# Moved scalings, reordered first transfers and products on ones in a two-layer hybrid decoder kernel

## The chip, the cores and the metric

The kernel runs on one core of one Trainium2 chip. The metric is the device time of one execution in microseconds (us); lower is better. A profiled execution also leaves a trace, whose span runs from the first to the last instruction.

## The reference

Two layers work on h, 272 tokens (16 learned ones and 256 of the input) by 2048 channels in float32:

```python
u = rmsnorm(h, pre_w)
proj = u @ w_in
pool_v, pool_g, z, xbc, dt, q, k, v, g, iq, ik, iw = split(proj)
pool_out = silu(pool_g) * pool_mixer(pool_v)            # windowed means, minus the input, grouped matmul
ssd_out = ssd_mixer(xbc, z, dt)                         # conv, chunked state space, y * silu(z), group norm
attn_out = silu(g) * dsa_attention(q, k, v, iq, ik, iw) # top-64 keys chosen by an index score
mix = concat([pool_out, ssd_out, attn_out])
h = h + rmsnorm(mix @ w_out, post_w)
```

The state-space mixer has 32 heads in 4 groups. Each group's y is gated and normalised by the mean of its squares. The output is the last 256 tokens.

## The kernel before

Channels lie on the 128 partitions and tokens along the free axis. Each weight tile comes by a transfer on SP's queue (`wr`, five buffers) and is split in two halves. For each half ACT writes a high part `wh` (`split`, line 238) and DVE the low part `wl` (line 247); TensorE then makes three products per piece of u, whose own high part is made by ACT (line 397) and low part by DVE (line 399). There are 10 buffers for high and 9 for low parts. The order of all engines' queues is the order in which the Python program issues instructions: every queue is first in, first out.

**The lead.** Layer 0 begins with eight rounds (`hh` 0 to 7) in `lead_0`. Each round multiplies one half quarter of u with three weight halves: a small block `gm` (6 products of 272 columns) and two index-query blocks `g0iq` (12 each of 256). The weight tiles are numbered as they are used: 0, 1, 2 for the first quarter, then 3 (small), 4 and 5 for the second, and so on. x comes in eight pairs of chunks (`load_x(i, k)` loads pair 2i + k/2), and `feed(p)` makes the u parts of pair p; `LEAD` says before which product each is issued. A weight transfer waits until the tile that had its buffer five tiles before has been split. When the lead is done the sums of squares, the row factor, the rotary embedding and the index keys follow in the shade of the next blocks.

**Ticks.** The blocks' products are the backbone. After each quarter of a block `tick()` advances every generator in `gens` by one step; a `yield n` makes a generator sleep for n ticks. Elementwise work is thus put between the products by hand. A block has four ticks of some 2.8 us.

**Index stage.** `EARLIEST` lists what is issued in successive ticks: `K`, `R` and `D` make the index key and bring its lower rows down, `L1` and `L0` (`keys_low`) make its parts, `a` (`iq_1`) evacuates an index-query block with a shuffle and a product (lines 477 and 478), `b`, `h`, `l` finish it, `P` are the score products (line 647).

**Attention head** (`head`): softmax of the two query blocks, after which POOL scales the first 16 columns, replicated, into `lr` (line 779) and the rest in place in `lg` (line 781); TensorE transposes both (lines 786 to 792).

**State-space groups.** A group has five blocks: two `xs`, one `BC`, two `z`, hence 20 ticks. `post_BC` transposes B, makes `bt` (lines 978, 984, 985), and a tick later multiplies it into the states `pst` (line 994); then four `decay` generators make `M` on DVE, ACT and POOL (lines 1016, 1022, 1029), which `ssd_y` needs for `py` (line 1049), after the products `ph` (line 1043). At the end of the group `post_z` sums the squares of y, waits `PNY` ticks, multiplies by ones (`pn`, line 1095), waits a tick, evacuates, waits `PGY` ticks, makes the inverse root on DVE (7 instructions), waits a tick, scales y (line 1104, four instructions), waits a tick and splits the result (`mix_out`). These steps run beside the next group's blocks.

**End.** `out_tokens` multiplies by w_out with tokens on partitions, four strips of 512 columns for each half of the tokens. `post` squares a strip on ACT and scales it on DVE; `finish` makes the root from the four sums and then, strip by strip, adds the residual and stores. The second half's last products are held back, so that the first half's end runs beside them.

Of the kernel before, what the change touches and what calls it, by code (L numbers as in the profile page):

```python
# [10 lines left out]
F32 = mybir.dt.float32  # L11
# [7 lines left out]
P = 128  # L19
# [18 lines left out]
class Plan:  # L38
# [48 lines left out]
QROT = (2, 3, 0, 1)  # L87
PVW = (2, 2, 2, 3)
PLQ, PLQ3 = 2, 4
KY, VEY = 2, 2  # L90

LEAD1 = {("m", 5): "a0", ("m", 7): "f"}
EARLIEST = (
    ("f g", "b0", "K R h0", "a1", "m D l0", "b1 L1", "t L0 h1 a2"),
    ("g", "K R", "b0", "m D h0", "l0 a1", "b1 L1", "t L0 h1 a2"),
)
INDEX = (
# [3 lines left out]
)  # L101
MY = 4
PNY, PGY = 2, 7
VY = 2
XY = 2
LEAD = (
    {(): "f0 s f1", (0, 1): "f2", (0, 2): "f3", (1, 1): "f4", (1, 3): "f5", (2, 2): "f6", (3, 1): "f7"},
)
RY = 4
NX = 4  # L110
# [13 lines left out]
def hybrid(ctx: ExitStack, tc: tile.TileContext, I, out, dbg=None, layers=2):  # L124
# [23 lines left out]
    def rep8(ap):  # L148

        return bc(ap[:, None, :], [ap.shape[0], 8, 16])  # L150

    def by8(ap):
        return ap.rearrange("p (e s) -> p e s", e=8)
# [144 lines left out]
    def rsqrt_v(y, v, w, p):  # L298
# [6 lines left out]
        V.scalar_tensor_tensor(p, p, Q[2], w, op0=OP.add, op1=OP.mult)  # L305
        V.scalar_tensor_tensor(y, p, Q[3], y, op0=OP.add, op1=OP.mult)

    warm = const.tile([P, 1], F32, name="warm")
    V.memset(warm, 0.0)
    A.activation(warm, warm, AF.Copy)  # L310
# [3 lines left out]
    def load_x(eng, i, k):  # L314
        eng.dma_start(hs[i // 2][:, 4 * (i % 2) + k:4 * (i % 2) + k + 2], I["xT"][i, :, k:k + 2])

    def load_half(i, h):

        if not h:
            raws[i] = wraw.tile([P, 4, 256 if i else P], F32, name=f"wr{i}", tag="wr")  # L320
        src = I["wi"][0, i - 1, 0] if i else I["wm"][0, 0]
        nc.sync.dma_start(raws[i][:, 2 * h:2 * h + 2], src[:, 2 * h:2 * h + 2])
        lpos[0] = max(lpos[0], i + 1)

# [2 lines left out]
    for h in range(2):  # L327
        for i in range(1 + NLEAD):
            load_half(i, h)
        if h == 0:  # L330
            load_x(nc.sync, 0, 2)
    nc.sync.dma_start(par[:, 0, 16:], I["par"][:, 0, 16:])
    nc.sync.dma_start(par[:, 1], I["par"][:, 1])
    for i in range(1, 4):
        load_x(nc.sync, i, 0)
        load_x(nc.sync, i, 2)
        load(min(RAWB, 3 + i))
    xpad = []
    for i in range(2):
        t = const.tile([P, 2, 16 + T], F32, name=f"xpad{i}")  # L340
# [4 lines left out]
    ikl = const.tile([P, T], F32R, name="ikl")  # L345
    cst = const.tile([P, 3, P], F32, name="cst")
    ident, tri, tri8 = (cst[:, i] for i in range(3))
    ones_r = const.tile([P, P], F32R, name="ones")
    ones = ones_r.bitcast(F32)
    G.memset(ones, 1.0)  # L350
    dtc = const.tile([P, 2, 2, 32], F32, name="dtc")
    pfix = const.tile([P, 4, 16], F32, name="pfix")
    xpi, xpdone = [0], set()
# [15 lines left out]
    def layer(L, hs):  # L369
# [91 lines left out]
        def early():  # L461

            nc.sync.dma_start(rope, I["rope"])
            if L == 0:
                nc.sync.dma_start(dtc, I["dtc"])
                nc.sync.dma_start(pfix, I["pfix"])
            nc.sync.dma_start(mb, I["mask"])
# [280 lines left out]
        def head(i, c, qr, qs):  # L748
# [27 lines left out]

            lr = pr.tile([P, 3, 128], F32, name="lr", tag="pair")
            for j, (a0, a1, n) in enumerate(segs):
                G.tensor_scalar(by8(lr[0:n, j]), rep8(lg[0:n, a0:a0 + 16]), nm[j][0:n], None, op0=OP.mult)
                if j < 2:  # L780
                    G.tensor_scalar(lg[:, a0 + 16:a1], lg[:, a0 + 16:a1], nm[j], None, op0=OP.mult)
            yield HY
# [282 lines left out]
        def post_z(i, ps):  # L1065
            g, j = i // 2, i % 2
            zg = yield from gate(ps, t0, ("z", i))
            s = sd[g]
            yg = s["yg"]
            for c in (2 * j, 2 * j + 1):  # L1070
                yield from until(f"M{g}_{c}")
            yield 1
            yo = pair("yo")
            ssd_y(g, j, yo)
            yield 1
            V.tensor_tensor(yg[:, 2 * j:2 * j + 2, 16:], yg[:, 2 * j:2 * j + 2, 16:], yo[:, :, 16:], op=OP.add)
            ysl = yg[:, 2 * j:2 * j + 2, t0:]
            V.tensor_tensor(ysl, ysl, zg[:, :, t0:T], op=OP.mult)
            q = pair("ysq")
            A.activation(q[:, :, t0:], ysl, AF.Square)  # L1080
            G.tensor_tensor(q[:, 0, t0:], q[:, 0, t0:], q[:, 1, t0:], op=OP.add)
            if j == 0:
                s["q"] = q
                done.add(f"q{g}")
                return
            done.add(f"y{g}")
            yield from until(f"q{g}")
            qs = pr.tile([P, 2, T], F32R, name="ysr", tag="pair")
            G.tensor_tensor(qs[:, 0, t0:], q[:, 0, t0:], s["q"][:, 0, t0:], op=OP.add)
            G.tensor_tensor(q[:, 0, t0:], q[:, 0, t0:], s["q"][:, 0, t0:], op=OP.add)  # L1090
            G.tensor_tensor(qs[:, 1, t0:], q[:, 0, t0:], qs[:, 0, t0:].bitcast(F32), op=OP.subtract)
            yield PNY
            pn = aux("pn")
            for k in range(2):
                TE.matmul(pn[:, t0:T], ones_r, qs[:, k, t0:], start=k == 0, stop=k == 1)
            yield 1

            rg, v, w_, p_ = (rope[:, k, t0:] for k in range(4))
            V.tensor_scalar(v, pn[:, t0:T], 1.0 / (512 * KQ * KQ), EPS / (KQ * KQ), op0=OP.mult, op1=OP.add)
            yield PGY  # L1100
            rsqrt_v(rg, v, w_, p_)
            yield 1
            for c in range(4):
                V.scalar_tensor_tensor(yg[:, c, t0:], yg[:, c, t0:], pa[:, NW + 4 * g + c:NW + 4 * g + c + 1], rg,
                                       op0=OP.mult, op1=OP.mult)
            dump_m(f"mixS{L}_{g}", yg)
            m = slots.tile([P, 2, 4, T], F32R, name=f"mixS{L}_{g}", tag=f"S{SS[g] if g < 3 else SP_[1]}")
            mixS[g] = m
            yield 1
            mix_out((m, 0), yg[:, :, t0:], t0, 4)  # L1110
            done.add(f"mixS{g}")
# [76 lines left out]
        def lead_0():  # L1188

            lead = [psg.tile([P, 2, 512], F32, name=f"g{L}iq{b}", tag="g") for b in range(2)]  # L1190
            pm = aux(f"gm{L}")
            row["ps"] = aux("psr")
            spawn(squares_0())

            def lead_in(*key):

                for w in LEAD[L].get(key, "").split():
                    if w == "s":
                        split(3, 3)
                    else:  # L1200
                        feed(int(w[1]))

            lead_in()
            for hh in range(8):
                q, half = hh // 2, hh % 2
                lead_in(hh, 0)
                gemm_h([pm], us[q], half, 0, q == 0, q == 3)
                for b in range(NLEAD):
                    lead_in(hh, 1 + b)
                    gemm_h(banks(lead[b]), us[q], half, NM, q == 0, q == 3)  # L1210
                lead_in(hh, 3)
                tick()
                if hh == 1:
                    nc.sync.dma_start(cst, I["cst"])
                if hh == 3:
                    early()
            misc["ps"] = pm
            for b in range(NLEAD):
                iqp[b] = lead[b]
            iq_1(0)  # L1220
            spawn(index_stage())
            spawn(dt_chain())
# [207 lines left out]
    def out_tokens(mixes, SO, SR, done, pool_mm):  # L1430
# [7 lines left out]
        def residual():  # L1438

            for p in range(8):  # L1440
# [8 lines left out]
                for b in range(2):  # L1449
                    A.copy(res[b][:, 256 * p:256 * p + 256], pt[:, 256 * b:256 * b + 256])  # L1450

        def post(n, b, ps):
            j = pair("osq")
            A.activation(j.rearrange("p c t -> p (c t)")[:, 0:512], ps, AF.Square, accum_out=ss[:, b, n:n + 1])
            V.scalar_tensor_tensor(o[b][:, 512 * n:512 * n + 512], ps, KQ * math.sqrt(DM),
                                   pw[n // 2][:, 512 * (n % 2):512 * (n % 2) + 512], op0=OP.mult, op1=OP.mult)

        def partial(b):

# [1 line left out]
            V.tensor_reduce(v, ss[:, b, 0:3], op=OP.add, axis=AX.X)  # L1461
            V.tensor_scalar(v, v, EPS * DM, None, op0=OP.add)

        def finish(b):
            y, v, w, p_ = (tot[:, b, i:i + 1] for i in range(4))
            V.tensor_tensor(v, v, ss[:, b, 3:4], op=OP.add)
            V.tensor_scalar(y.bitcast(I32), v.bitcast(I32), -0.5, RSQ, op0=OP.mult, op1=OP.add)
            V.scalar_tensor_tensor(w, y, y, v, op0=OP.mult, op1=OP.mult)
            V.scalar_tensor_tensor(p_, w, Q[0], w, op0=OP.add, op1=OP.mult)
            V.scalar_tensor_tensor(p_, p_, Q[1], w, op0=OP.add, op1=OP.mult)  # L1470
            V.scalar_tensor_tensor(p_, p_, Q[2], w, op0=OP.add, op1=OP.mult)
            V.scalar_tensor_tensor(y, p_, Q[3], y, op0=OP.add, op1=OP.mult)
            for c0, c1 in ((0, 512), (512, 1024), (1024, 1536), (1536, 2048)):
                x = o[b][:, c0:c1]
                V.scalar_tensor_tensor(x, x, y, res[b][:, c0:c1], op0=OP.mult, op1=OP.add)
                nc.sync.dma_start(out[b, :, c0:c1], x)

        HOLD = HIB - 1
        for n in range(4):
# [32 lines left out]
                continue  # L1512
            while gens:
                tick()
            post(3, 0, o_[0])
            finish(0)
            for i, h in enumerate(held):
                mm_t(o_[1], *h, False, i == len(held) - 1)
            post(3, 1, o_[1])
            finish(1)  # L1520

    split_h = []

# [81 lines left out]
```

## Time and profile before

| | |
|---|---|
| median of 3 runs | 1556.72 us (1556.2 to 1557.01) |
| profiled execution, its own time | 1555.74 us |
| its span | 1554.0 us |
| TensorE busy | 1528.7 us (98%) |
| DVE busy | 1209.7 us (78%) |
| ACT busy | 889.2 us (57%) |
| POOL busy | 229.3 us (15%) |

The span holds all instructions; the 1.7 us around it belong to the execution but to no instruction. Busy shares are means over stages with different limits. A wait in the trace is the idle time of an engine before an instruction, put down to what ended it.

### The profile page before, as it was taken

What the parts mean: (1) busy time and instruction counts of PE and PEld (TensorE: products, weight loads), DVE (VectorE), ACT (ScalarE), POOL (GpSimd) and SP (SyncE); (2) the same over time, 40 slices, a digit from 0 to 9 for tenths busy, and PEclk for the clock granted to TensorE, in tenths of its full rate; (3) what the DMA queues carried; (4) which work ended last, traced back from release to release, by engine and by line L of the source; (5) the groups of instructions that cost most, each with busy time, mean ns of one, the idle gap of its engine ahead of it and who ended that gap; (6) DMA issues with size and microseconds to landing.
All of it is one profiled execution on the core that took longest, in us unless ns stands there. A gap on an engine that the chain in (4) does not pass through costs nothing.

```text
span 1554.0 us, 31057 instructions
## 1 busy us (share of the span) xinstructions
PE 1528.7 (98%) x11788; PEld 1472.2 (95%) x11788; DVE 1209.7 (78%) x2370; ACT 889.2 (57%) x1667; POOL 229.3 (15%) x227
## 2 busy tenths in 40 slices
PE   7999999999999999999999999999999999999997
PEld 7999999999999999999999999999999999988886
DVE  6989777788899978554599898877898989875454
ACT  6455556666667664444455545666667667445542
POOL 0000253221203031000100000532103021300000
PEclk9999999999999999999999999999999999999999
DMA  8545543455454545555536546545454554466652
GB/s 278 192 151 166 174 150 136 158 173 190 136 179 153 189 156 174 206 201 177 176 110 246 180 142 205 162 151 175 167 192 147 194 183 159 164 229 199 217 185 92
DMA packets 78310, 272.44 MB, mean 175 GB/s; under 512 B 8848, under 2 KB 11984, under 8 KB 77136
## 3 DMA queue, kind: packets, MB, share of 16 engines
q1 hardware_dynamic: 78064, 270.39, 51.8%
q8 instruction: 92, 1.51, 0.4%
q14 instruction: 58, 0.48, 0.1%
q10 hardware_dynamic: 96, 0.07, 0.0%
HBM read 266.03 MB, written 4.40 MB: 174 GB/s over the span
## 4 chain that ended last, share of the span: by engine, by line
PE 91%; DVE 4%; issue 2%; POOL 1%; DMA 1%; SPq 0%; ACT 0%; DVEq 0%; ACTq 0%; POOLq 0%
PE go L274 4%; PE go L273 4%; PE go L272 4%; PE got L296 4%; PE got L294 4%; PE got L295 4%; PE g0xs L272 2%; PE g1xs L272 2%; PE g0xs L274 2%; PE g1xs L274 2%; PE g0xs L273 2%; PE g1xs L273 2%; PE g1z L272 2%; PE g1z L274 2%; PE g1z L273 2%
## 5 line engine op out<-in xcount | busy, mean ns | idle before, releaser
L247 DVE TENSOR_TENSOR wl<-wr,wh 128x512 fp32r<-128x512 f32 (+1 forms) x952 | 664.2, 724 | 251.3 <-PE go L274 66.2
L238 ACT CAST wh<-wr 128x512 fp32r<-128x512 f32 (+1 forms) x952 | 564.8, 615 | 404.9 <-PE go L273 88.1
L272 PE MATMUL g0xs<-u,wh 128*128 128x272 f32 x256 | 74.7, 292 | 0.0
L272 PE MATMUL g1xs<-u,wh 128*128 128x272 f32 x256 | 74.6, 291 | 0.0
L272 PE MATMUL g0z<-u,wh 128*128 128x272 f32 x256 | 74.5, 291 | 0.0
L274 PE MATMUL go<-mixS,wl 128*128 128x272 f32 x256 | 74.1, 290 | 0.0
L274 PE MATMUL g0xs<-u,wl 128*128 128x272 f32 x256 | 74.1, 290 | 0.0
L274 PE MATMUL g0z<-u,wl 128*128 128x272 f32 x256 | 74.1, 289 | 0.0
L274 PE MATMUL g1xs<-u,wl 128*128 128x272 f32 x256 | 74.0, 289 | 0.0
L272 PE MATMUL go<-mixS,wh 128*128 128x272 f32 x256 | 74.0, 289 | 0.0
L273 PE MATMUL g0xs<-u,wh 128*128 128x272 f32 x256 | 73.6, 288 | 0.0
L273 PE MATMUL g1xs<-u,wh 128*128 128x272 f32 x256 | 73.6, 287 | 0.0
L273 PE MATMUL go<-mixS,wh 128*128 128x272 f32 x256 | 73.6, 287 | 0.0
L273 PE MATMUL g0z<-u,wh 128*128 128x272 f32 x256 | 73.6, 287 | 0.0
L272 PE MATMUL g1z<-u,wh 128*128 128x256 f32 x256 | 72.7, 284 | 0.0
L274 PE MATMUL g1z<-u,wl 128*128 128x256 f32 x256 | 71.6, 280 | 0.0
L273 PE MATMUL g1z<-u,wh 128*128 128x256 f32 x256 | 71.6, 280 | 0.0
L1029 POOL TENSOR_TENSOR M<-M,cbm 128x512 f32<-128x512 f32 x32 | 50.9, 1591 | 93.0 <-ACT M L1022 93.0
L484 POOL TENSOR_TENSOR ropet<-ropet,rope 128x544 f32<-128x544 f32 (+1 forms) x8 | 10.6, 1327 | 353.0 <-DVE ropet L477 353.0
L1016 DVE TENSOR_SCALAR M<-csb,cs 128x128 f32<-128x128 f32 x128 | 50.9, 446 | 0.0
L294 PE MATMUL got<-wh,mixS 128*128 128x512 f32 x128 | 50.8, 397 | 0.0
L296 PE MATMUL got<-wh,mixS 128*128 128x512 f32 x128 | 50.5, 394 | 0.0
(525 smaller groups left out, 5357.8 us busy)
## 6 DMA issues: line engine op xcount, KB each, us to landing
wr<-wi SPq DMA_DIRECT2D x334, 512.0 KB, 3.3
wr<-wo SPq DMA_DIRECT2D x128, 512.0 KB, 3.4
csb<-csd SPq DMA_DIRECT2D x8, 1088.0 KB, 8.5
x<-xT SPq DMA_DIRECT2D x8, 272.0 KB, 4.7
res<-xT SPq DMA_DIRECT2D x4, 544.0 KB, 6.4
h1d<-o SPq DMA_DIRECT2D x4, 544.0 KB, 6.8
wr<-plw SPq DMA_DIRECT2D x8, 256.0 KB, 2.7
hx<-h1d SPq DMA_DIRECT2D x8, 256.0 KB, 3.7
```

What stands on the lines that cost most here:

```text
L238: A.copy(hi, r[:, 2 * h:2 * h + 2])
L247: V.tensor_tensor(lo, r[:, 2 * h:2 * h + 2], his[i].bitcast(F32), op=OP.subtract)
L272: TE.matmul(o, w_h, u[:, 0, k, t1:T], start=first and k == 0, stop=False)
L273: TE.matmul(o, w_h, u[:, 1, k, t1:T], start=False, stop=False)
L274: TE.matmul(o, w_l, u[:, 0, k, t1:T], start=False, stop=last and k == 3)
L294: TE.matmul(o, m_h, hi, start=first, stop=False)
L295: TE.matmul(o, m_h, lo, start=False, stop=False)
L296: TE.matmul(o, m_l, hi, start=False, stop=last)
L484: e.tensor_tensor(t[:, :nch, c0:T], t[:, :nch, c0:T], bc(rope[:, b + 1:b + 2, c0:T], [P, nch, n]), op=OP.mult)
L1016: V.tensor_scalar(M[:, h, sl], csb[:, h, sl], cs[:, 1 + b, hg:hg + 1], 0.0, op0=OP.subtract, op1=OP.min)
L1029: G.tensor_tensor(M[:, hh, 16:], M[:, hh, 16:], bc(cbm[:, None, 16:], [P, 2, 256]), op=OP.mult)
```

## The change

- Ten products of a 128x128 tile of ones with itself are issued on TensorE first; the tile is made by POOL's first instruction.
- The first transfers come in another order: tiles 3 and 4 come in halves as tiles 0 to 2 do, each pair of x just ahead of its halves; `par`'s larger pieces go behind `rope` in `early()`; pairs 5, 6 and 7 are issued with the parts of `LEAD`, behind tiles 5, 6 and 7.
- In `EARLIEST` `L0` moves one step ahead of `a2`, and `L1` ahead of `b1`.
- The replicated columns `lr` are scaled by DVE instead of POOL.
- `PNY` is 3 instead of 2. `PGY` is 6 instead of 7 for the first three groups and 3 for the last; the scaling then waits 3 ticks (1 for the last) instead of 1. In ticks after the sums of squares: `pn` at 3 (was 2), root at 10 (was 10), scaling at 13 (was 11), split at 14 (was 12); for the last group root at 7, scaling at 8, split at 9.
- At the end the last strip is scaled after the root, just before it is added, and in two halves for the second half of the tokens; the squares are summed as before.

```diff
+WARM = 10
 EARLIEST = (
-    ("f g", "b0", "K R h0", "a1", "m D l0", "b1 L1", "t L0 h1 a2"),
-    ("g", "K R", "b0", "m D h0", "l0 a1", "b1 L1", "t L0 h1 a2"),
+    ("f g", "b0", "K R h0", "a1", "m D l0", "L1 b1 L0", "t h1 a2"),
+    ("g", "K R", "b0", "m D h0", "l0 a1", "L1 b1 L0", "t h1 a2"),
 )
-PNY, PGY = 2, 7
+PNY, PGY, SGY = 3, 6, 3
 LEAD = (
-    {(): "f0 s f1", (0, 1): "f2", (0, 2): "f3", (1, 1): "f4", (1, 3): "f5", (2, 2): "f6", (3, 1): "f7"},
+    {(): "f0 s f1", (0, 1): "f2 x5", (0, 2): "f3 x6 x7", (1, 1): "f4", (1, 3): "f5", (2, 2): "f6", (3, 1): "f7"},
 )
+    ones_r = const.tile([P, P], F32R, name="ones")
+    ones = ones_r.bitcast(F32)
+    G.memset(ones, 1.0)
+
+    pw_ = aux("warm")
+    for _ in range(WARM):
+        TE.matmul(pw_[:, 0:P], ones, ones, start=True, stop=True)
...
-    nc.sync.dma_start(par[:, 0, 16:], I["par"][:, 0, 16:])
-    nc.sync.dma_start(par[:, 1], I["par"][:, 1])
-    for i in range(1, 4):
-        load_x(nc.sync, i, 0)
-        load_x(nc.sync, i, 2)
-        load(min(RAWB, 3 + i))
+    for h in range(2):
+        load_x(nc.sync, 1, 2 * h)
+        for i in range(1 + NLEAD, RAWB):
+            load_half(i, h)
+    load_x(nc.sync, 2, 0)
...
             nc.sync.dma_start(rope, I["rope"])
             if L == 0:
+                nc.sync.dma_start(par[:, 0, 16:], I["par"][:, 0, 16:])
+                nc.sync.dma_start(par[:, 1], I["par"][:, 1])
...
-                G.tensor_scalar(by8(lr[0:n, j]), rep8(lg[0:n, a0:a0 + 16]), nm[j][0:n], None, op0=OP.mult)
+                V.tensor_scalar(by8(lr[0:n, j]), rep8(lg[0:n, a0:a0 + 16]), nm[j][0:n], None, op0=OP.mult)
...
-            yield PGY
+            yield PGY if g < 3 else 3
             rsqrt_v(rg, v, w_, p_)
-            yield 1
+            yield SGY if g < 3 else 1
...
+        def square_t(k, b, ps):
+            j = pair("osq")
+            A.activation(j.rearrange("p c t -> p (c t)")[:, 0:ps.shape[1]], ps, AF.Square, accum_out=ss[:, b, k:k + 1])
+
+        def scale_t(b, ps, c0):
+            c1 = c0 + ps.shape[1]
+            V.scalar_tensor_tensor(o[b][:, c0:c1], ps, KQ * math.sqrt(DM),
+                                   pw[c0 // 1024][:, c0 % 1024:(c1 - 1) % 1024 + 1], op0=OP.mult, op1=OP.mult)
...
-            for c0, c1 in ((0, 512), (512, 1024), (1024, 1536), (1536, 2048)):
+            for c0, c1, ps in strips:
+                if ps is not None:
+                    scale_t(b, ps, c0)
                 x = o[b][:, c0:c1]
...
-            post(3, 0, o_[0])
-            finish(0)
+            whole = [(c, c + 512, None) for c in range(0, 1536, 512)]
+            square_t(3, 0, o_[0])
+            finish(0, 3, whole + [(1536, 2048, o_[0])])
...
-            post(3, 1, o_[1])
-            finish(1)
+            square_t(3, 1, o_[1])
+            finish(1, 3, whole + [(1536, 1792, o_[1][:, 0:256]), (1792, 2048, o_[1][:, 256:512])])
```

## Rows read from the trace of the kernel before

**Rows 1.** The page's first part: busy us (share of the span) xinstructions.

```profile
PE 1528.7 (98%) x11788; PEld 1472.2 (95%) x11788; DVE 1209.7 (78%) x2370; ACT 889.2 (57%) x1667; POOL 229.3 (15%) x227
```

**Rows 2.** Waits of PE: who waited for whom: us in total, times, longest.

```profile
PE gm L272 <- ACT wh L238: 5.9, 1, 5.9
PE pst L994 <- DVE bt L984: 5.4, 6, 1.3
...
PE pt L791 <- POOL lg L781: 0.9, 2, 0.5
PE pq L647 <- DVE ikl L524: 0.6, 1, 0.6
...
PE g1k L272 <- DVE iqr L478: 0.4, 1, 0.4
PE pq L647 <- DVE iqr L478: 0.4, 1, 0.4
PE pn L1095 <- POOL ysr L1091: 0.3, 1, 0.3
```

**Rows 3.** Stretches: length, busy us (xcount) of each engine, clock, DMA share, GB/s.

```profile
5.90:10.70 4.80, 4.76 (x22) 4.77 (x23) 3.62 (x7) 3.78 (x8) 0.00 (x0) 1.00 1.06 381
10.70:17.50 6.80, 6.80 (x58) 6.76 (x57) 3.46 (x7) 2.63 (x7) 0.00 (x0) 1.00 1.03 396
17.50:20.10 2.60, 0.67 (x4) 0.30 (x2) 1.54 (x4) 2.60 (x7) 0.00 (x0) 1.00 0.35 139
20.10:24.40 4.30, 4.28 (x23) 4.28 (x24) 4.10 (x9) 3.76 (x9) 0.00 (x0) 0.60 0.63 158
24.40:40.80 16.40, 16.40 (x139) 16.40 (x139) 14.82 (x27) 12.23 (x24) 0.00 (x0) 1.00 0.85 301
```

**Rows 4.** Timeline: start, us, engine, line, instruction, count [idle before]; the sixth tile.

```profile
17.48 0.62 ACT L238 CAST wh<-wr 128x512 fp32r<-128x512 f32 x1 [2.10 <-DMA wr<-wi]
...
19.39 1.02 DVE L247 TENSOR_TENSOR wl<-wr,wh 128x512 fp32r<-128x512 f32 x2
...
20.12 0.39 PE L274 MATMUL g0iq<-u,wl 128*128 128x256 f32 x1 [1.47 <-DVE wl L247]
```

**Rows 5.** Timeline of DVE and PE where the second layer's second group makes states.

```profile
1161.41 1.67 DVE L1104 SCALAR_TENSOR_TENSOR yg<-yg,par,rope 128x256 f32<-128x256 f32 x4
...
1163.10 0.28 PE L274 MATMUL g1z<-u,wl 128*128 128x256 f32 x1
...
1164.33 0.29 DVE L984 TENSOR_TENSOR bt<-pb,bt 32x128 fp32r<-32x128 f32 x1
...
1164.67 0.50 PE L994 MATMUL pst<-xdd,bt 128*128 128x512 f32 x1 [1.29 <-DVE bt L984]
```

**Rows 6.** Timeline of DVE and PE at the second layer's first score products.

```profile
854.36 0.66 DVE L478 TENSOR_TENSOR iqr<-g1iq,rope 128x512 f32<-128x512 f32 x1
...
855.16 0.36 PE L272 MATMUL g1k<-u,wh 128*128 128x272 f32 x1 [0.44 <-DVE iqr L478]
```

**Rows 7.** Timeline of POOL in an attention head of the second layer.

```profile
1007.61 1.66 POOL L779 TENSOR_SCALAR lr<-lg,nm 128x128 f32<-128x128 f32 x1
1009.25 0.92 POOL L781 TENSOR_SCALAR lg<-lg,nm 128x256 f32<-128x256 f32 x1
```

**Rows 8.** Timeline of DVE, POOL and PE among a group's decays in the second layer.

```profile
1172.43 1.80 DVE L1016 TENSOR_SCALAR M<-csb,cs 128x128 f32<-128x128 f32 x3
...
1172.65 1.31 POOL L1029 TENSOR_TENSOR M<-M,cbm 128x512 f32<-128x512 f32 x1 [5.61 <-ACT M L1022]
...
1183.86 1.28 POOL L1029 TENSOR_TENSOR M<-M,cbm 128x512 f32<-128x512 f32 x1 [3.45 <-ACT M L1022]
...
1188.78 0.61 PE L1043 MATMUL ph<-BC,H 128*128 128x128 f32 x4
```

**Rows 9.** Timeline of DVE at the end.

```profile
1545.58 0.69 DVE L1455 SCALAR_TENSOR_TENSOR ot<-got,pw 128x512 f32<-128x512 f32 x1 [1.50 <-ACT osq L1454]
...
1547.59 2.74 DVE L1475 SCALAR_TENSOR_TENSOR ot<-ot,tot,rt 128x512 f32<-128x512 f32 x4
```

More of the change, by code (lines that the diff above doesn't have):

```diff
@@ L317, in load_half @@
     def load_half(i, h):
+        q, b = divmod(i, 1 + NLEAD)
         if not h:
-            raws[i] = wraw.tile([P, 4, 256 if i else P], F32, name=f"wr{i}", tag="wr")
-        src = I["wi"][0, i - 1, 0] if i else I["wm"][0, 0]
+            raws[i] = wraw.tile([P, 4, 256 if b else P], F32, name=f"wr{i}", tag="wr")
+        src = I["wi"][0, b - 1, q] if b else I["wm"][0, q]
         nc.sync.dma_start(raws[i][:, 2 * h:2 * h + 2], src[:, 2 * h:2 * h + 2])
@@ L347, in hybrid @@
     ident, tri, tri8 = (cst[:, i] for i in range(3))
-    ones_r = const.tile([P, P], F32R, name="ones")
-    ones = ones_r.bitcast(F32)
-    G.memset(ones, 1.0)
     dtc = const.tile([P, 2, 2, 32], F32, name="dtc")
@@ L1199, in lead_in @@
                         split(3, 3)
+                    elif w[0] == "x":
+                        load_x(nc.sync, int(w[1]) // 2, 2 * (int(w[1]) % 2))
                     else:
@@ L1450, in residual @@
                     A.copy(res[b][:, 256 * p:256 * p + 256], pt[:, 256 * b:256 * b + 256])
+        def square_t(k, b, ps):
[5 more added lines that the diff above has]
+                                   pw[c0 // 1024][:, c0 % 1024:(c1 - 1) % 1024 + 1], op0=OP.mult, op1=OP.mult)
         def post(n, b, ps):
[L1453 to L1456, printed above, removed]
+            square_t(n, b, ps)
+            scale_t(b, ps, 512 * n)
         def partial(b):
@@ L1462, in partial, with finish @@
             V.tensor_scalar(v, v, EPS * DM, None, op0=OP.add)
-        def finish(b):
+        def finish(b, k, strips):
             y, v, w, p_ = (tot[:, b, i:i + 1] for i in range(4))
-            V.tensor_tensor(v, v, ss[:, b, 3:4], op=OP.add)
+            V.tensor_tensor(v, v, ss[:, b, k:k + 1], op=OP.add)
             V.tensor_scalar(y.bitcast(I32), v.bitcast(I32), -0.5, RSQ, op0=OP.mult, op1=OP.add)
```

## The prediction

> **What bounds the kernel now.** I read the page first: TensorE is busy 98% of the span and DVE 78% [rows 1]. A busy matmul row includes overlapped time, so I didn't read this as "nothing left"; I asked where TensorE stands still. The list of its waits has nine rows, some 16 us in all; the two of the lead are told by the timeline below, the others are [rows 2]: 5.9 before the first product, 5.4 in six waits of the state product `pst`, and under 1 us each at the head transposes `pt`, the score products `pq`, `g1k` and `pn`. The reader should see that every edit aims at one of these rows.
>
> The waits hide a second loss, the pace. By stretch [rows 3], the lead took 22 matmuls in 4.80 us at first (0.218 us each), 58 in 6.80 (0.117), 23 in 4.30 at a granted clock of 0.60, then 139 in 16.40 (0.118). The first stretch ran at the lower level (1.2 GHz) by its pace, whatever its clock column says (no record stands so early), and the third again mostly at that level, just after 2.60 us in which TensorE was busy for 0.67. The lead's 240 products (8 rounds of 30) take 240 x 0.118 = 28.3 us at the full pace; they took 34.9 (5.9 to 40.8). So 6.6 us are the most that the lead can give.
>
> Why it stood still is in the timeline [rows 4]. ACT waited 2.10 us for a weight transfer and split it at 17.48; the two parts of u that stand next in ACT's and DVE's queues went ahead of its low half, which DVE began at 19.39; TensorE went on at 20.12. DMA was full meanwhile (396 GB/s, share 1.03 [rows 3]), so that transfer was late because of what stood ahead of it.
>
> **Part by part: the start.** The late transfer is the sixth weight tile (`wr5`, block iq1 of the second quarter). Today two pieces of `par` and three x pairs go ahead of it that the change puts behind it: 0.19 MB and 3 x 0.279 MB, 1.03 MB in all. At 396 GB/s that is 2.6 us. Its issue doesn't hold it back: it waits for the buffer of tile 0, whose last reader is among the first splits. So ACT's split moves from 17.48 to about 14.9, and with the same steps behind it (2.64 us from 17.48 to 20.12) TensorE goes on at 17.5. If it then keeps the higher level, the 23 matmuls of 20.1 to 24.4 take 23 x 0.118 = 2.7 instead of 4.3: 1.6 more. DVE's chain moves by 2.6 only and TensorE's by 4.2; I take 0.1 off for low halves that are now just in time: 4.1 us. Bounds: 2.6 (the lower level returns) and 6.6 (no loss at all).
>
> The ten products on ones leave two records each. Four f32 128x128 products are 0.61 us [rows 8], so 20 records are about 3.0 us, some 5.6 at the lower level's pace; begun near 1 us they end, at the worst, 0.7 after the first real product could start (5.9). I cost them at nothing and also give them nothing. With a fast first round TensorE reaches the sixth tile at most 2.2 earlier (22 x 0.1), near 15.3 to 16, and waits there 1.5 to 2.2; with a slow one it arrives near 17.5, as today. Either way it goes on at 17.5. The transfer covers gain and cost; without that cover they would be worth up to 2.2.
>
> On SP the pairs x5, x6, x7 now queue behind tiles 5, 6 and 7, which wait for buffers. Their u parts are used two and more rounds of 3.6 us later; that covers them. The two `par` pieces now go behind `rope`: nothing of them is read in the lead. `rope` keeps its place; weight tiles issued after them are later by two issues, covered by the splits that run ahead.
>
> **Keys.** `keys_low(0)` goes ahead of the ring's next shuffles, and one of the score waits names `ikl`. In the second layer [rows 2, 6] `pq` waits 0.6 for `ikl`, then `g1k` 0.4 for `iqr` L478, the evacuation whose bank it takes: that ends at 854.36+0.66 = 855.02 and `g1k` starts at 855.16. L478 stays behind the same DVE work, only in another order, so it ends when it does today. `pq` gets earlier and `g1k` waits for longer. In the first layer `pq` itself waits for L478 (0.4). So I take 0; bounds 0 and 1.9 (three waits gone, 0.6 + 0.4 + 0.4 + 3 x 0.16).
>
> **Scaling of y.** In the second layer four scalings (1.67 us from 1161.41) stand in DVE's queue ahead of the work whose end `pst` awaits: 1163.10, the last product; 1164.33+0.29 = 1164.62, `bt`; 1164.67, `pst` [rows 5]. Start to start that is 1.57 where 0.12 is the step: 1.45 lost, 0.16 more than the row's 1.29 (it counts from the modelled end). The change puts the scaling two ticks later, behind `pst`. DVE's chain then ends 1.67 earlier, at 1162.95, before 1163.22: the wait goes, with 0.27 to spare. The first layer's waits are shorter (5.4 less 3 x 1.3 leaves 1.5 for its three) and go too. Six waits: 5.4 + 6 x 0.16 = 6.4 us. Bounds 3.2 and 6.4.
>
> What is late next: the scaling (1.7) and, a tick later, the low part of the mix (1.2) now stand among the decays. The fourth `M` product on POOL ends at 1183.86+1.28 = 1185.14; `py` needs it after the `ph` products, at 1189.39 [rows 8]. That is 4.2 of cover, 2.8 after TensorE has gained 1.45; the delay is 2.9 at most, less the 1.7 and 1.2 taken away earlier in the same queue, about 0. Low halves of weights have the same net. yg's single buffer is next written three ticks after its last read.
>
> One row speaks against it: DVE's three `M` subtractions took 1.80 us where POOL ran a product (1172.65 to 1173.96) [rows 8], and `bt` of the same width 0.29 [rows 5]. DVE stood still beside POOL, and the scalings are moved among such products. Counted as work alone the move costs nothing; if each scaling is held, it costs what the last rival below says. The Trainium skill ("SBUF — State Buffer", "SBUF: two separate sides") has DVE and GpSimd share a pair of ports as an exclusive lock, the loser blocked for the whole instruction; the row agrees with it, and by it alone the last rival would be the forecast.
>
> **lr on DVE.** POOL takes 1.66 and 0.92 for the last two [rows 7]; TensorE waits for the last. Without the `lr` POOL is done some 1.6 to 3 earlier, over the wait of 0.9 in two (0.9 + 2 x 0.16 = 1.2). DVE gets two or three scalings of 128x128 for each head, at 0.3 (`bt` [rows 5]) to 0.6 each (1.80 / 3 [rows 8]), behind the reciprocals that it does anyway, and POOL, done sooner, stands less in its way. 1.2; bounds 0 and 1.2.
>
> **Sums of squares** one tick later: `pn`'s 0.3 goes, 0.5 start to start; bounds 0 and 0.5. For the last group the root and scaling come three ticks earlier, into the pool blocks where DVE has idle time: 0.
>
> **Tail.** After the last square the first scaling (0.69 at 1545.58) leaves the path ahead of the root; the four strips (2.74) [rows 9] and their stores start some 0.6 earlier, and the last scaling comes back in two halves. DVE's sum is 0.2 longer, the last store half as large and no longer behind a full one. I take 0.4; bounds -0.2 and 0.6.
>
> **Sum:** 4.1 + 0 + 6.4 + 1.2 + 0.5 + 0.4 = 12.6. The profiled execution took 1555.74 (span 1554.0 and 1.7 around it); it becomes 1543.1. The median of the runs is 1.0 above it, 1556.72: **1544.1**.
>
> **Rivals.**
> - The waits go as above: 1544.1, own range 1542.5 to 1545.5. Chance 0.51.
> - The clock falls again. If the products on ones have lifted it, TensorE then waits 1.5 to 2.2 for the sixth tile, and the standstill of 1.93 (2.60 less 0.67) was followed by the lower level [rows 3]; against it, the new one may be the shorter. Lead 2.6: 1545.6. Chance 0.17. The Trainium skill ("TensorE: Matmul & The Clock Gate", "What's actually happening") says that the lower clock is the idle default, that activity lifts it, and that the moment varies between runs of one kernel; by that rule this case could come in some runs and not in others, and the two slow stretches, each behind an idle one, agree with it.
> - DVE gives back half of y: the spare is 0.3 us, and low weight halves get tighter. 1544.1 + 3.2 = 1547.3. Chance 0.13.
> - The keys pay too: if `pq` and `g1k` get other banks, up to 1.9 more: 1542.2. Chance 0.09.
> - The new transfer order does not do what it says: x5 to x7 behind buffer waits come as late as the sixth tile did. Lead 0: 1548.2. Chance 0.06; rows show no such queue.
> - Slower: the four scalings in each of six groups meet POOL's `M` products. If each is held about 1 us (the 1.80 for three [rows 8]), and the mix's 1.2 comes on top, `M` ends 4 x 1.0 + 1.7 + 1.2 = 6.9 later, 4.1 past its cover of 2.8, 6 times: 24.6 lost, 1568.7. It decides from 2.1 us past the cover (12.6 / 6). Against it: a blocked DVE only waits out a POOL product that some DVE instruction there waits out already. Chance 0.04.
>
> **Range.** 1541.0 to 1549.0 leaves out the last and the edges of the others, under 2 in 10. A measurement of this kernel tells about 0.2%, 3.1 us, from no change: faster 0.93 (all but the last, less a little for mixtures), same 0.03, slower 0.04.
>
> **What the new profile would show.** ACT's split of the sixth tile near 14.9, with TensorE idle before it and on at 17.5; the second lead block (`g0iq2`) begun near 36.7, not 40.8; no second stretch at the lower clock; no `pst`, `pt` or `pn` wait of size; a wait for `iqr` L478 still at `pq` and `g1k`; the first store 0.6 after the square's end sooner. I am wrong if `pst` still waits for `bt`, if `wl` waits appear behind the scalings, or if the sixth tile lands no earlier.

## The result, and the profile after

The changed kernel takes 1545.16 us in the median of four runs (1544.77 to 1547.09), the kernel before 1556.74 beside it: ratio 0.9929, 95% interval 0.9911 to 0.9946. That is 11.6 us less, where 12.6 were forecast. The profiled execution took 1545.04 (span 1543.3), 10.7 less in span than before. The two differences are 0.9 apart because the kernel before was profiled in an execution 1.0 faster than its median, the changed kernel in one 0.1 faster. Against the traces the forecast is 1.9 too large: one term is offset by a loss that was not in the forecast, others came out larger.

The page's first part, as in [rows 1]; TensorE's 20 more matmuls are the products on ones:

```profile
PE 1527.5 (99%) x11808; PEld 1472.1 (95%) x11808; DVE 1212.8 (79%) x2412; ACT 885.9 (57%) x1667; POOL 196.6 (13%) x187
```

The waits of PE, all of them, against [rows 2]:

```profile
PE g0iq L275 <- DVE wl L248: 1.5, 2, 1.2
PE g1k L273 <- DVE iqr L485: 1.2, 1, 1.2
PE px L933 <- ACT xr L914: 1.2, 4, 0.3
PE gm L273 <- ACT wh L239: 1.0, 1, 1.0
PE warm L315 <- POOL ones L311: 1.0, 1, 1.0
PE pq L654 <- DVE iqr L485: 0.8, 1, 0.8
PE g1iq L275 <- DVE wl L248: 0.2, 1, 0.2
```

`pst`, `pt` and `pn` are gone. `pq`'s wait for `ikl` is gone too, and `g1k`'s for `iqr` has grown by about as much. Two rows were not foreseen: `px`, the transposes of the next group's `xs`, waits four times for ACT's copy `xr`, and `g1iq` waits 0.2 for a low half. `warm` is the first of the products on ones; they run from 0.97 to 4.98, ahead of the first real product at 5.96.

The lead by stretch, columns as in [rows 3]:

```profile
5.90:10.70 4.80, 4.52 (x33) 4.16 (x34) 3.61 (x7) 4.15 (x9) 0.00 (x0) 1.00 1.02 366
10.70:15.00 4.30, 4.30 (x38) 4.30 (x37) 3.37 (x7) 2.25 (x6) 0.00 (x0) 1.00 1.05 403
15.00:17.70 2.70, 1.46 (x13) 1.26 (x11) 1.57 (x4) 2.65 (x7) 0.00 (x0) 1.00 1.05 399
17.70:20.40 2.70, 2.70 (x22) 2.70 (x23) 2.44 (x6) 1.97 (x6) 0.00 (x0) 1.00 0.63 180
20.40:37.00 16.60, 16.60 (x140) 16.47 (x139) 14.22 (x26) 12.24 (x26) 0.00 (x0) 1.00 0.83 292
```

The first stretch holds 33 matmuls where there were 22, and the 22 behind the sixth tile take 2.70 at a granted clock of 1.00, where 23 took 4.30 at 0.60. The timeline of the sixth tile, answering to [rows 4]:

```profile
15.05 0.62 ACT L239 CAST wh<-wr 128x512 fp32r<-128x512 f32 x1 [1.55 <-DMA wr<-wi]
...
16.13 0.92 DVE L404 SCALAR_TENSOR_TENSOR u<-x,par,u 128x272 fp32r<-128x272 f32 x2 [1.67 <-ACT u L402]
...
16.96 1.02 DVE L248 TENSOR_TENSOR wl<-wr,wh 128x512 fp32r<-128x512 f32 x2
...
17.70 0.39 PE L275 MATMUL g0iq<-u,wl 128*128 128x256 f32 x1 [1.24 <-DVE wl L248]
```

Split at 15.05 (forecast 14.9), on at 17.70 (17.5). The second layer's second group, DVE, POOL, ACT and PE, answering to [rows 5, 8]:

```profile
1156.39 0.29 DVE L991 TENSOR_TENSOR bt<-pb,bt 32x128 fp32r<-32x128 f32 x1
...
1156.88 0.40 PE L1001 MATMUL pst<-xdd,bt 128*128 128x512 f32 x1
...
1160.77 1.66 DVE L1111 SCALAR_TENSOR_TENSOR yg<-yg,par,rope 128x256 f32<-128x256 f32 x4
...
1162.95 0.86 DVE L1023 TENSOR_SCALAR M<-csb,cs 128x128 f32<-128x128 f32 x4
...
1164.94 1.21 DVE L620 TENSOR_TENSOR mixS<-yg,mixS 128x1024 fp32r<-128x1024 f32 x1
...
1165.71 1.59 POOL L1036 TENSOR_TENSOR M<-M,cbm 128x512 f32<-128x512 f32 x1 [6.62 <-ACT M L1029]
...
1166.08 1.90 DVE L1023 TENSOR_SCALAR M<-csb,cs 128x128 f32<-128x128 f32 x4
...
1194.97 0.50 ACT L914 COPY xr<-xs 128x128 f32<-128x128 f32 x2
...
1195.32 0.33 PE L933 MATMUL px<-cst,xr 128*128 128x128 f32 x1 [0.29 <-ACT xr L914]
```

`bt`'s first part is ready at 1156.68 and `pst` follows the product before it without a gap. The scaling stands behind `pst`, the low part of the mix between the first two decays. Then the first score products of the second layer, answering to [rows 6], and DVE at the end, to [rows 9]:

```profile
849.55 0.67 DVE L485 TENSOR_TENSOR iqr<-g1iq,rope 128x512 f32<-128x512 f32 x1
...
850.37 0.36 PE L273 MATMUL g1k<-u,wh 128*128 128x272 f32 x1 [1.25 <-DVE iqr L485]
...
1535.07 0.16 DVE L1483 TENSOR_TENSOR tot<-tot,ss 128x1 f32<-128x1 f32 x1 [1.37 <-ACT osq L1463]
...
1536.48 2.08 DVE L1494 SCALAR_TENSOR_TENSOR ot<-ot,tot,rt 128x512 f32<-128x512 f32 x3
```

**The ledger.** I took the start of the same matmul in both traces and noted where the distance between them changes (the wait rows are smaller, since they count from modelled ends):

| term | forecast | measured | where |
|---|---|---|---|
| lead | 4.1 | 3.8 | `psr` (sums of squares, behind the lead) 43.65 to 39.88 |
| keys | 0 | -0.2 | `pq` and `g0k` of the first layer -0.2; second layer +0.74 at `pq`, -0.74 at `g1k` |
| scaling of y | 6.4 | 6.7 | six `pst`: 0.76, 0.68, 0.72, then 1.56, 1.51, 1.47 |
| the same, given back | 0 | -1.8 | four `px`, 0.45 to 0.48 each |
| `lr` | 1.2 | 1.5 | `pt` 0.73 and 0.81 |
| `pn` | 0.5 | 0.9 | mostly behind the last group of each layer |
| low half in the second lead | - | -0.4 | `g1iq` at 832.7 |
| tail | 0.4 | 0.2 | 9.5 us from the last product's start to the end became 9.3 |
| sum | 12.6 | 10.7 | spans 1554.0 and 1543.3 |

### The profile page after: what moved, and what is told of

Same layout as the page of the kernel before. It is cut to its first block, busy times and chain, and to the rows that moved or that the text cites. A ratio compares the mean times of both kernels' runs of the same rounds, so it can differ in the third digit from the quotient of the medians.

```text
span 1543.3 us, 31074 instructions
## 1 busy us (share of the span) xinstructions
PE 1527.5 (99%) x11808; PEld 1472.1 (95%) x11808; DVE 1212.8 (79%) x2412; ACT 885.9 (57%) x1667; POOL 196.6 (13%) x187
## 4 chain that ended last, share of the span: by engine, by line
PE 94%; DVE 3%; DMA 1%; ACT 1%; issue 1%; SPq 0%; DVEq 0%; ACTq 0%
PE go L275 4%; PE go L274 4%; PE go L273 4%; PE got L297 4%; PE got L295 4%; PE got L296 4%; PE g0z L273 2%; PE g0z L275 2%; PE g0z L274 2%; PE g1z L273 2%; PE g1z L275 2%; PE g0xs L273 2%; PE g1z L274 2%; PE g1xs L273 2%; PE g1xs L275 2%; PE g0xs L275 2%
## 5 line engine op out<-in xcount | busy, mean ns | idle before, releaser
L248 DVE TENSOR_TENSOR wl<-wr,wh 128x512 fp32r<-128x512 f32 (+1 forms) x952 | 652.6, 714 | 244.8 <-PE go L275 66.8
```

The lines of the kernel that those rows point to most:

```text
L248: V.tensor_tensor(lo, r[:, 2 * h:2 * h + 2], his[i].bitcast(F32), op=OP.subtract)
```

## The experiments

All against the changed kernel's 1545.16. Executions of one kernel differ by up to 3.4 us (run 10), and each kernel left one trace. Nine traces have the same lead in their code, those of the changed kernel and of runs 3 to 6, 8 to 10 and 12: `psr` starts between 39.86 and 42.06 in them, latest in run 4, where the granted clock fell behind the sixth tile. So a single trace tells the worth of an edit in the lead to some 2 us only; the stages behind the lead are read from the traces.

**1. Without the products on ones.** `-WARM = 10` / `+WARM = 0`

> The changed kernel (1545.2 us) without the ten products on ones. In its trace TensorE waits 1.4 us for the sixth weight tile, from 16.2 to 17.7. Theory (the prediction): the products are covered; the first round is slow again and TensorE arrives about 1.3 us later (what the first round gained), near 17.5, and still goes on near 17.7, as DVE ends that low half. Time 1545.2 to 1545.6; the pace after 17.7 stays that of the higher level, since there is no standstill left. Rival A: the 1.3 us of the first round were a gain of their own: 1546.5. Rival B: without the early work the lower level comes back after the sixth tile as in the kernel before (1.4 us for 23 matmuls): 1546.6 to 1548.

1546.99 (1545.81 to 1547.06); ratio to before 0.9937 (0.9925 to 0.9949). In the profiled execution (span 1544.0) the first round is 1.3 slower than in the changed kernel's trace, TensorE waits 1.19 in place of 1.40 and goes on at 18.06 in place of 17.70; a further low half costs 0.4 near 25, and `psr` starts at 40.78, 0.9 later. The clock did not fall behind the sixth tile. But the nine traces with the products on ones spread as widely: TensorE goes on between 17.70 and 18.59 in them, `psr` starts between 39.86 and 42.06, and in runs 3, 6 and 10 the first round is 1.4 slower than here, because part of it ran at the lower clock level. This is that stretch of run 3:

```profile
8.50:11.90 3.40, 3.40 (x19) 3.40 (x18) 2.74 (x7) 3.26 (x8) 0.00 (x0) 0.50 1.04 370
```

The intervals of the two kernels' times overlap too. What the products on ones are worth beside the new order is not shown: neither the theory nor rival A is settled.

**2. First transfers in the old order.**

```diff
+    nc.sync.dma_start(par[:, 0, 16:], I["par"][:, 0, 16:])
+    nc.sync.dma_start(par[:, 1], I["par"][:, 1])
+    for i in range(1, 4):
+        load_x(nc.sync, i, 0)
+        load_x(nc.sync, i, 2)
+        load(min(RAWB, 3 + i))
-    for h in range(2): ...
-    {..., (0, 1): "f2 x5", (0, 2): "f3 x6 x7", ...}
+    {..., (0, 1): "f2", (0, 2): "f3", ...}
```

> The changed kernel with the first transfers in the old order (both pieces of par and three x pairs ahead of the sixth tile), the products on ones kept. Theory: the sixth tile lands and is split as before (ACT at 17.5, low half on DVE at 19.4), TensorE arrives near 16.2, waits 3.9 us and goes on at 20.1: 2.4 us lost, and after such a standstill the next 23 matmuls run at the lower level, 1.4 more: 1549.0, the whole gain of the lead (3.8). Rival A: the products on ones keep the level up, only 2.4 is lost: 1547.6. Rival B: the order is not what moved the tile: 1545.2.

1550.16 (1548.16 to 1551.02). The sixth tile is split at 18.21, where it was 15.05, and TensorE goes on at 20.85:

```profile
18.21 0.62 ACT L239 CAST wh<-wr 128x512 fp32r<-128x512 f32 x1 [2.07 <-DMA wr<-wi]
```

```profile
18.00:20.85 2.85, 0.86 (x6) 0.46 (x4) 1.57 (x4) 2.64 (x7) 0.00 (x0) 1.00 0.31 119
20.85:25.30 4.45, 4.45 (x24) 4.45 (x25) 4.07 (x9) 4.40 (x11) 0.00 (x0) 0.62 0.59 151
```

The standstill and the 24 matmuls at 0.62 behind it are like those of [rows 3]. The lead loses 4.5, more than the 3.8 it had gained (and 0.8 more goes at a low half in the second layer's lead): the order is what moved the tile. With the old order the products on ones kept nothing in this trace: its lead is 0.7 longer than that of the kernel before.

**3. The scaling of y back at its place.** `-SGY = 3` / `+SGY = 1` (ticks between root and scaling).

> The changed kernel with the scaling of y (and its mix behind it) two ticks sooner, where it was before; sums of squares stay a tick later. In the changed kernel's trace the six pst waits are gone (6.1 us start to start), and px has four new waits for the xr copy (1.8 us, in the second and third change of group of each layer). Theory: the mix between the decays holds DVE and ACT some 0.9 us back up to xr, so px waits because of the scaling: with the scaling back, pst waits return and px waits go: 6.1 - 1.8 = 4.3 more, 1549.5. Rival: px waits because pn now stands a tick later, just ahead of it; they stay, 6.1 more: 1551.3.

1550.45 (1550.17 to 1551.48): 5.3 more. The waits of PE hold

```profile
PE pst L1001 <- DVE bt L991: 5.4, 6, 1.3
```

again and no row of `px`. From the lead's end on this trace loses 4.9: six `pst`, less four `px` got back. The `px` waits belong to the scaling, not to `pn`'s place, which was kept.

**4. The scaling one tick later in place of two.** `-SGY = 3` / `+SGY = 2`

> The changed kernel with the scaling of y one tick later than before in place of two: on DVE it stands behind bt and ahead of the state sum, and the mix ahead of the first decay in place of among them. Theory: pst stays free (its operands are still ahead of the scaling), the decays behind the first come some 1 us sooner, and the four px waits (1.8 us) go: 1543.4. Rival A: px waits because of pn's place: no change, 1545.2. Rival B: the scaling meets bt and the pst waits come back in part (up to 1.3 each in three): 1547 to 1549.

1545.57 (1545.06 to 1546.79): no gain. `pst` stays free. In the first layer the two `px` waits shrink from 0.43 to 0.17 each (too short for the list of waits, but `px` still starts 0.05 behind the end of the copy), in the second both stay (0.51 each): there the scaling and the mix now stand ahead of the state sum on DVE, which starts 6.6 behind `pst` in place of 5.5, and the second decay is no sooner (9.2 behind `pst` in both). At which of these two places ahead of the last decay the work stood made no difference to `xr` in the second layer. The profiled execution (1546.79) shows something else, with the same code in its lead as the changed kernel:

```profile
16.80:18.56 1.76, 0.29 (x2) 0.08 (x1) 1.57 (x4) 1.76 (x6) 0.00 (x0) 1.00 0.90 344
18.56:22.80 4.24, 4.24 (x22) 4.24 (x23) 4.08 (x9) 4.24 (x10) 0.00 (x0) 0.60 0.56 169
```

Here the clock did fall behind the wait for the sixth tile, which costs 4.24 - 2.70 = 1.5.

**5. The low part of the mix behind the last decay** (the 3 is a constant `MLY` in the kernel).

```diff
-            mix_out((m, 0), yg[:, :, t0:], t0, 4)
+            A.copy(m[:, 0, :, t0:], yg[:, :, t0:])
+            yield 3 if g < 3 else 0
+            V.tensor_tensor(m[:, 1, :, t0:], yg[:, :, t0:], m[:, 0, :, t0:].bitcast(F32), op=OP.subtract)
```

> The changed kernel with DVE's low part of the mix (1.2 to 1.3 us) three ticks later, behind the last of the four decays of its group in place of among them; the scaling and ACT's high part stay. Theory: from the state sum to the last decay DVE has no idle time (each decay is held 1.3 us beside a POOL product), so work put in there makes everything behind it later, up to xr; behind the last decay DVE idles 1 to 2 us. The decays come about 1 us sooner and all four px waits (1.8 us) go, in the second layer too, where the scaling one tick sooner left them: 1545.2 - 1.8 = 1543.4. Rival: px waits because TensorE itself gained 0.7 to 1.5 per group and pn stands in front of it: unchanged, 1545.2. In all these runs the lead (the first 40 us) differs by up to 2 us between executions by the granted clock, so the stages behind it are read from the trace.

1543.70 (1543.35 to 1543.84). The timeline:

```profile
1164.51 0.86 DVE L1023 TENSOR_SCALAR M<-csb,cs 128x128 f32<-128x128 f32 x4
...
1174.32 1.21 DVE L1119 TENSOR_TENSOR mixS<-yg,mixS 128x1024 fp32r<-128x1024 f32 x1
...
1193.47 0.50 ACT L914 COPY xr<-xs 128x128 f32<-128x128 f32 x2
...
1194.41 0.27 PE L933 MATMUL px<-cst,xr 128*128 128x128 f32 x1
```

The second decay's four subtractions, 1.90 beside POOL's product above, now come before it and take 0.86. `xr` ends at 1193.97, ahead of `px`; all four waits are gone, 2.0 start to start when counted to the last product of `px` (1.8 at its first, as in the ledger). Theory confirmed, in both layers.

**6. The evacuation first.** `-"L1 b1 L0", "t h1 a2"` / `+"L1 a2 L0 b1", "t h1"`, both layers.

> The changed kernel with the evacuation of iq2 (a2) put ahead of the shuffle's second half (b1) and of the other low keys, in both layers. Theory (the prediction's reason for giving the keys nothing): pq (1.0 us, first layer) and g1k (1.45, second layer) wait for that evacuation alone; it ends about 2 us sooner, both waits go: 2.4 less, 1542.8. Rival A: the low keys, now behind it, become the last wait at pq: less than 1 us of gain, 1544.4. Rival B: the bank isn't what they wait for: 1545.2.

1543.10 (1542.69 to 1543.62). The waits of PE, whole but for the lead's:

```profile
PE px L933 <- ACT xr L914: 1.2, 4, 0.3
...
PE g1iq L275 <- DVE wl L248: 0.3, 1, 0.3
```

`pq` starts 1.1 sooner (0.16 of it lost again at the next one) and `g1k` 1.2: 2.2 of the 2.4.

**7. A part of u later in the lead.** `-(1, 1): "f4"` / `+(1, 2): "f4"`

> The changed kernel with the fifth part of u (f4) made one block later in the lead, so that DVE takes the sixth tile's low half before it. In the changed kernel's trace ACT's split of that tile ends at 15.7, DVE stands idle until 16.1 for the part of u and takes the low half only at 16.96; TensorE waits 1.4 us until 17.70. Theory: that wait is no longer the transfer's but DVE's order; the low half ends near 16.4 and TensorE goes on at 16.5: 1.2 less, 1544.0, and with hardly a standstill there the granted clock doesn't fall behind it. Rival A: the tile behind it (the next low half) is late by as much, so the wait moves there: 1545.2. Rival B: the transfer still decides: 1545.2, wait at the same place.

1545.98 (1545.46 to 1548.34): nothing gained. The wait at the sixth tile falls to 0.3 (start to start) and 0.6 appears at a later low half (20.33): rival A, the wait moved on. In its profiled execution `pq` of the first layer stood for 1.9 (1.0 in the changed kernel's; why is open), and the clock fell there too (23 matmuls in 3.80 at 0.55).

**8. `lr` back on POOL.** `-V.tensor_scalar(by8(lr` / `+G.tensor_scalar(by8(lr`

> The changed kernel with the scalings lr back on POOL. Theory: the two pt waits of the second layer return, 0.6 to 0.8 us each start to start: 1.4 to 1.5 more, 1546.7. Rival: with the other changes POOL is early enough and DVE is relieved of the lr: nothing, 1545.2.

1547.28 (1547.04 to 1549.30). The row is back, 1.4 start to start. The trace is 1.9 longer; the other 0.5 lies at the low half in the second layer's lead:

```profile
PE pt L798 <- POOL lg L788: 0.9, 2, 0.5
```

**9. Both edits that paid (5 and 6).**

> The changed kernel with both edits that paid: the low part of the mix behind the last decay and the evacuation of iq2 ahead of the other shuffles. Theory: their waits are in different stages and add up: 2.0 (px) and 2.4 (pq, g1k) less than the changed kernel, 1545.2 - 4.4 = 1540.8. Rival: TensorE, earlier by 4.4, meets the next late low halves (the wl wait in the second layer's lead is 0.4 to 0.9 now and would grow): 1541.5 to 1542.5.

1541.41 (1541.20 to 1541.76), ratio to before 0.9899 (0.9885 to 0.9912): the best, 3.75 below the changed kernel and 15.3 below the one before. Its waits of PE, all:

```profile
PE g0iq L275 <- DVE wl L248: 1.5, 2, 1.2
PE warm L315 <- POOL ones L311: 1.0, 1, 1.0
PE g0iq L273 <- ACT wh L239: 0.8, 1, 0.8
PE g1iq L275 <- DVE wl L248: 0.2, 1, 0.2
```

Beyond the lead, one wait of 0.2 is left. `px` (2.0), `pq` (0.9) and `g1k` (1.4) add up to 4.3; the lead of this execution was 0.65 longer.

**10. Splits one half further ahead.** To 9, in the last four steps of the second layer's lead: `+ahead[0] = min(ahead[0] + 0.25, HIB)`

> The one with both edits, and the splits of weights run one half further ahead from the last four steps of the second layer's lead on. Theory: the wl wait there (0.4 to 0.9 us, behind the eight DVE instructions of the row root) goes, since DVE is idle 1.4 us just before them: 0.4 to 0.9 less than with both edits, 1540.2. Rival: weight tiles aren't there that early or the splits crowd out the shuffles behind them: no change or 0.5 slower.

1543.86 (1542.99 to 1546.43): 2.4 slower, the rival and worse. ACT's timeline, and two stretches:

```profile
828.74 2.40 ACT L239 CAST wh<-wr 128x512 fp32r<-128x512 f32 x4 [1.42 <-DMA wr<-wi]
```

```profile
831.80:834.30 2.50, 0.36 (x4) 0.15 (x3) 2.40 (x6) 0.00 (x0) 0.00 (x0) 0.99 0.04 15
834.30:838.20 3.90, 3.79 (x14) 2.81 (x15) 3.31 (x9) 1.30 (x3) 0.00 (x0) 0.57 0.49 139
```

The half asked for sooner waits for its transfer on ACT, the row root now queues behind its low half on DVE, and the low half that TensorE needs queues behind the root. TensorE waits 2.3 in place of 0.4 and then runs at a lower clock.

**11. The lead's order too.** To 10: the fifth x pair issued behind the sixth tile, and edit 7.

> The same with the lead changed too: the fifth x pair issued behind the sixth weight tile, and its part of u one block later. Theory: the tile lands 0.7 us sooner and DVE takes its low half first, so that TensorE's wait of 1.4 us in the lead goes, and the wait for the next low half that the later part of u alone brought (0.6) is smaller as the whole row of splits is sooner: 0.7 to 1.4 less, 1539.2. Rival: the lead is bound by the sum of transfers and splits, not by their order, so the wait only moves to the next tiles: no change.

1543.62 (1542.76 to 1544.77). Against 10 the time gains nothing that counts, and the loss of 10 is still in it, so that it can't be compared with 9. The trace tells of the lead: TensorE goes on at the sixth tile at 16.73, 1.0 sooner than in the changed kernel's, and 0.8 of that is lost again at the next low half (19.79). That is the rival: the wait moves. `psr` starts at 39.61, only 0.25 ahead of the earliest of the nine traces.

**12. Low keys in the old order.** `-"L1 b1 L0", "t h1 a2"` / `+"b1 L1", "t L0 h1 a2"`

> The changed kernel with the low keys in the old order. Theory (the prediction): the edit is worth nothing alone; in the second layer pq's wait for ikl returns (0.7) and g1k's wait for iqr shrinks by as much (1.45 to 0.65), in the first pq still waits for iqr: 1545.2. Rival: the low keys were worth their pq wait: 1545.9 or more.

1545.49 (1545.23 to 1546.25). The rows of [rows 2] are back:

```profile
PE pq L654 <- DVE ikl L531: 0.6, 1, 0.6
...
PE g1k L273 <- DVE iqr L485: 0.4, 1, 0.4
PE pq L654 <- DVE iqr L485: 0.4, 1, 0.4
```

`pq` of the second layer is 0.75 later, `g1k` 0.02 (0.74 got back). As forecast, the edit moves a wait and saves nothing.

## Why the prediction was right

1545.16 lies in the likeliest case's own range, in part by luck: the trace gained 10.7 where 12.6 were forecast, and the medians came nearer (11.6) only by where the profiled executions fell. By its steps:

- **Start.** The mechanism holds: the sixth tile is split 2.4 sooner (15.05 for 17.48), TensorE goes on 2.4 sooner (17.70 for 20.12), and 1.4 more comes from the higher clock behind it; 3.8 for 4.1. Run 2 shows that the order did it. The size had luck: 3.8 is the upper end of the nine traces with this lead (1.6 to 3.8, mean 3.3), and "either way it goes on at 17.5" came out as 17.70 to 18.59. A slow first round is mostly covered: in runs 3, 6 and 10 it ended 2.0 later than in the changed kernel's trace, and `psr` came 0.3 to 0.7 later. The products on ones took 4.0 for the 3.0 worked out and still ended ahead of the first real one.
- **The clock rival** (0.17) is real. In the changed kernel's trace the clock held behind the wait, in run 4's, with the same lead, it fell, for 1.5. The Trainium skill ("TensorE: Matmul & The Clock Gate", "What's actually happening") has the point at which the clock changes vary from run to run; the nine traces of this lead agree, since part of the first round ran at the lower level in three of them, the products behind the sixth tile in run 4, and neither in the other five.
- **Keys.** 0 was right (-0.2 measured), for the reason given: L485 (L478 before) is the last wait at both places. Run 6 moved it and got the 2.2 that the edit left.
- **Scaling of y.** The six `pst` waits went as worked out (6.7 for 6.4). The step that failed is the cover behind them: the prediction held the queue's delay, "about 0", against POOL's last product and `py`, and stopped there; 1.8 was lost at a later reader, `px`. The delay itself was sized well. In the second layer's second group the trace comes in 6.3 sooner than before; the fourth `M` product then ends 6.4 sooner, and `xr` starts 6.6 sooner (1194.97 for 1201.61), since the moved work stood ahead of `xr` before the change too. But with the `pst` wait gone TensorE comes to `px` 7.9 sooner, 1.2 more than `xr`. `py` had cover for that. In the kernel before, `px` had 0.85 of cover, since the first of the two copies, 0.30 long, ended at 1201.91:

```profile
1201.61 0.50 ACT L907 COPY xr<-xs 128x128 f32<-128x128 f32 x2
...
1202.76 0.27 PE L926 MATMUL px<-cst,xr 128*128 128x128 f32 x1
```

Now it keeps 0.05, so that some 0.45 is lost. This is the rival in which DVE gives back half of y (3.2), at 1.8 and at a reader that I hadn't named. Run 3 shows that the waits come with the scaling's new place, run 5 that 1.2 less work on DVE ahead of `xr` removes them.

- **The slower rival** didn't come. Among the decays of the six groups none of the scalings met a POOL product; in the group shown they took 1.66 for four, 1.67 before [rows 5]. What met one were the decays' own subtractions, as before: 21 of 128 took some 1.3 in place of 0.27 in both traces, as the argument against this rival had it. Behind the last group of each layer, where the root and the scaling come three ticks earlier, three of the four scalings did meet POOL's products:

```profile
586.21 4.25 POOL L1142 TENSOR_TENSOR pw<-pw 128x568 f32<-128x568 f32 x3
...
586.61 4.57 DVE L1111 SCALAR_TENSOR_TENSOR yg<-yg,par,rope 128x272 f32<-128x272 f32 x4
```

They took 4.57 in place of 1.8. TensorE lost nothing by it, so the 0 there came out right, but not because DVE was undisturbed. The Trainium skill ("SBUF — State Buffer", "SBUF: two separate sides") has the pair of ports that DVE and POOL (GpSimd) share as an exclusive lock, held for a whole instruction; these rows agree.

- **`lr`** 1.5 for 1.2 (1.4 in run 8) and **`pn`** 0.9 for 0.5: each wait is worth more start to start than its row says; the 0.16 that I added, taken from `pst`, was too little at `pt`. **Tail** 0.2 for 0.4: the first strip came 0.6 sooner behind the square, as foreseen (1.44 for 2.05). With the two late scalings DVE still ended 0.4 later behind it (5.2 for 4.8), where 0.2 was worked out; the last store, half as large, landed 1.9 after its issue in place of 2.7. No run tests `pn` or the tail by itself.
- **Not foreseen:** 0.4 at a low half in the second layer's lead, where the kernel before lost 0.03. It was 0.4 to 1.1 in the runs that keep the order of the splits there; what sets it is open, beyond that the row root stands ahead of it on DVE.

## What to carry to other kernels

When a wait goes, the engine that waited comes sooner to every later reader of the same queue, and each of them needs cover, not only the first. Here TensorE, 1.5 sooner, passed one reader with 2.7 to spare and waited 38 us behind `pst` at one that had had 0.85. An edit at a wait that only hands over to the next wait is worth nothing until the last one is moved. Running ahead more can put an instruction that waits for a transfer in front of one that is needed now. One trace of a stage whose clock varies is one draw: nine traces of the same lead ended 2.2 us apart.

## What the runs showed of the hardware

A wait of TensorE in an otherwise busy stretch was in some traces followed by the lower granted clock. At the sixth tile a wait of 1.6 us (start to start) was, in the kernel before and in runs 2 and 4 (0.60, 0.62 and 0.60 in the next stretch, mostly the lower level of 1.2 GHz); waits of 1.5 in run 5 and 1.6 in run 12 were not. Waits of 1.9 in run 7 and 2.3 in run 10 were (0.55 and 0.57), the three of 1.45 at `pst` in the kernel before were not, and in runs 3, 6 and 10 the clock fell within the first round behind waits of at most 1.2. So the length of the wait alone did not decide. Such a wait can cost twice its row: in run 4 it was followed by 1.5 more.

DVE stood still beside POOL's products: a decay's subtraction of 128x128 took some 1.3 where it met one and 0.27 where it didn't, a scaling of 128x272 1.4 to 1.6 for 0.5.
